# Ranks of weight splits and output sums, the first weights' engines, the attention output loads and three buffers of a hybrid decoder layer

## The chip, the cores and the metric

The kernel runs on one core of one Trainium2 chip. The metric is the device time of one execution in microseconds (us); the time before is the median of three runs. Engines are named as in the profile: PE (TensorE matmuls, PEld its weight loads), DVE (VectorE), ACT (ScalarE), POOL (GpSimd), SP (SyncE, which issues nearly all DMAs).

## What is computed

One decoder layer on 1024 tokens of width 1024, in float32:

```
h = rmsnorm(x); proj = h @ w_in
fox:  8 heads x 64, causal softmax(q k / 8 + F[t] - F[s]) v,  F = cumsum(log sigmoid(f + bias))
sb:   8 heads x 64, weights sigmoid(z) * prod over s<j<t of (1 - sigmoid(z_j)),  z = q k / 8, s < t
x = x + [rmsnorm(o_fox), rmsnorm(o_sb)] @ w_out
u = causal depthwise conv (width 3) of rmsnorm(x) @ w_up;  gate, val = split(u)
x = x + (silu(gate) * val) @ w_down;  out = rmsnorm(x)
```

## The kernel before, in words

Everything is held transposed, features on the 128 partitions and tokens along the row. A float32 operand is split into a rounded high part and the rest (`hi`, `lo`), and each product is three matmuls (`mm3`, L159 to L162): high by high, and the two mixed ones.

**Order of work.** Tile's scheduler orders the instructions of PE, DVE, ACT and POOL from their ranks (their place in the program, unless a rank is given) and its own estimate of when each can start. The order of SP is that of the program. Each engine then runs its list strictly in order; the chip's times only decide how long each entry waits.

**Start** (span 0 to 45 us). Eight 128x1024 blocks of x are loaded (`xr`), ACT makes their high part `xh` (L352) and squares them (L358, L361), DVE makes the low part `xl` (L353) and adds the squares to `sqa` (L362). PE multiplies them with the first two weight units (`w_qk[0]`, `w_qk[1]`, in four pieces each) into four PSUM banks of 12 matmuls per block; column sums of `sqa` (L180) give the norm `rst` and, spread over the rows (L185), `rbc`. `constants()` makes an identity and two masks on POOL, cast by DVE (L87, L93, L96); the second mask is written over the first one's tile.

**Weights.** Class `W` (L124 on) loads a unit into one of two `wraw` buffers and splits it piece by piece: high part on POOL (L142), low part on POOL (L144), or ACT and DVE for units with `act=True` (the last of w_out and the first of w_up). `wspl` has three pairs for the results.

**Attention** (45 to 650 us) goes head by head, in the order p, hb; `attention_stream` issues the scores, transposes and value products of a head, and between them `fill_stream` issues projection work for later heads (`v_quarter`, `qk_unit`) at a fixed rate. A head's q, k high, k low and v come back from DRAM in `load_head` (L432, L435) and `load_v` (L440) one head ahead. In a fox head DVE combines scores with a row `fbt` (L476), ACT exponentiates (L486) and POOL scales (L490). In a stick-breaking head ACT takes two sigmoids (L481 into `qt`, L482), DVE scans `qt` backwards (L494), POOL multiplies (L495). The two `qt` tiles come from the pool of the `fbt` rows (two buffers), and POOL sets their last column (L460). `finish` (L540 on) stores a pair's output to `od` and adds its squares to `oacc` on POOL (L555).

**Output projection.** After the last unit (p = 7) `open_out` (L620 on) spreads the fox norm, and loads the four fox outputs back through `load_og`: a load into a buffer `oraw` (L613; tag `hl`, two buffers, shared with the projection's `hl`), a high part on ACT (L617), a low part on DVE (L618). After a pause of 12 units of the fill's clock `fox_out` (L641 on) multiplies them with w_out while the last heads run; per row block m it loads a block of x into `xin` (L646; also tag `hl`), and DVE scales, adds (L653, L654) and stores (L655). Then come the rest of the output projection, the norm, the two large products of the feed-forward part (650 to 1400 us) and the last norm.

Of the kernel before, what the change touches and what calls it, by code (L numbers as in the profile page):

```python
# [9 lines left out]
F32 = mybir.dt.float32  # L10
# [3 lines left out]
ALU = mybir.AluOpType  # L14
# [3 lines left out]
P = 128  # L18
D = 1024
T = 1024  # L20
# [32 lines left out]
ORDER, ORDER_LAST = (0, 1, 3, 2), (0, 1, 3, 2)  # L53
LAG, LEAD, RATE, PAUSE, TRC = 3, 40.0, 1.327, 12.0, 0.67
UA = 3

PARTS = ((0, 512), (512, 256), (768, 256))
NORM_AT = ((1, 3), (2, 3), (3, 0))
# [5 lines left out]
def f32(ap):  # L64
    return ap.bitcast(F32)
# [3 lines left out]
def layer(ctx, tc, xT, wqk, wv0, wv, wout, wup, wdn, cols, fbias, yT):  # L69
# [44 lines left out]
    class W:  # L114
# [16 lines left out]
        def split(self, upto):  # L131
            if self.done == 0 and upto > 0:
                self.dma()
                self.hi = self.pool.tile([P, self.n if self.own else 1056], F32R, name=self.tag + "h")
                self.lo = self.pool.tile([P, self.n if self.own else 1056], F32R, name=self.tag + "l")
            while self.done < upto:
                q = self.n // self.pieces
                sl = slice(self.done * q, (self.done + 1) * q)
                if self.act:
                    nc.scalar.copy(self.hi[:, sl], self.raw[:, sl])  # L140
                else:
                    nc.gpsimd.tensor_scalar(self.hi[:, sl], self.raw[:, sl], 1.0, 0.0, ALU.mult, ALU.add)  # L142
                eng = nc.vector if self.act else nc.gpsimd
                eng.tensor_tensor(self.lo[:, sl], self.raw[:, sl], f32(self.hi[:, sl]), ALU.subtract)  # L144
                self.done += 1

        def get(self):
# [248 lines left out]
    ps_s = attn.enter_context(tc.tile_pool(name="ps_s", bufs=3, space=PSUM))  # L396
    ps_t = attn.enter_context(tc.tile_pool(name="ps_t", bufs=2, space=PSUM))
    ps_o = attn.enter_context(tc.tile_pool(name="ps_o", bufs=1, space=PSUM))
    NQ = 2
    oacc = bcp.tile([P, T], F32, name="oacc")  # L400
    qi = []
# [48 lines left out]
    def score(p, hb, i, ws):  # L450
        fox = p < NFOX
        q, kh, kl, vt, fbt = heads[p, hb]
        n = (i + 1) * P
        w = pp.tile([P, T], F32, name="w")
        ws[i] = w
        m = None
        if not fox:
            if len(qi) < NQ:
                qi.append(fp.tile([P, T + 1], F32, name="fbt"))
                nc.gpsimd.memset(qi[-1][:, T:T + 1], 1.0)  # L460
            qt = qi[count[0] % NQ]
            count[0] += 1
        for c0, cn in CHUNKS[i]:
            s = ps_s.tile([P, 512], F32, name="s")
            qb = q[:, i * P:(i + 1) * P]
            diag = c0 <= i * P < c0 + cn
            nc.tensor.matmul(s[:, :cn], qb, kh[:, c0:c0 + cn], start=True, stop=False)  # L467
            nc.tensor.matmul(s[:, :cn], qb, kl[:, c0:c0 + cn], start=False, stop=not diag)
            if diag:
                o = i * P - c0  # L470
                nc.tensor.matmul(s[:, o:o + P], identb, mask_f if fox else mask_s,  # L471
                                 start=False, stop=True)
            un = min(cn, n - c0)
            if fox:
                m2 = small.tile([P, 1], F32, name="m")
                nc.vector.tensor_tensor_reduce(  # L476
                    out=w[:, c0:c0 + un], in0=s[:, :un], in1=fbt[:, c0:c0 + un], scale=-1.0,
                    scalar=3.0e38 if m is None else m, op0=ALU.add, op1=ALU.min, accum_out=m2)
                m = m2
            else:  # L480
                act(qt[:, T - n + c0:T - n + c0 + un], s[:, :un], AF.Sigmoid, scale=-1.0)  # L481
                act(w[:, c0:c0 + un], s[:, :un], AF.Sigmoid)  # L482

        if fox:
            l = small.tile([P, 1], F32, name="l")
            act(w[:, :n], w[:, :n], AF.Exp, scale=-1.0, bias=m, accum_out=l)  # L486

            def rest():
                nc.vector.reciprocal(l, l)  # L489
                nc.gpsimd.tensor_scalar(w[:, :n], w[:, :n], l, 1.0, ALU.mult, ALU.mult)  # L490
        else:
            def rest():
                rev = slice(T - 1, T - n - 1 if n < T else None, -1)
                nc.vector.tensor_tensor_scan(qt[:, rev], qt[:, rev], qt[:, rev], 1.0, ALU.mult, ALU.bypass)  # L494
                nc.gpsimd.tensor_tensor(w[:, :n], w[:, :n], qt[:, T - n + 1:T + 1], ALU.mult)  # L495
        defer(0, rest)
# [42 lines left out]
    def finish(p):  # L539
        ot = heads["o", p]  # L540
        g = 0 if p < NFOX else 1

        def go():
            if p < NPAIR - 1:
                nc.sync.dma_start(od[p], ot)
            else:
                load_og(p)
            if p % NFOX == 0:
                act(oacc, ot, AF.Square)
                return  # L550
            sq = pp.tile([P, T], F32, name="osq", tag="w")
            act(sq, ot, AF.Square)
            eng = nc.vector if p == NPAIR - 1 else nc.gpsimd
            for sl in (slice(0, 512), slice(512, T)):
                eng.tensor_tensor(oacc[:, sl], oacc[:, sl], sq[:, sl], ALU.add)  # L555
            if p == NFOX - 1:
                defer(12, partial(sums, oacc, ps_p, "pj"))
            elif p == NPAIR - 1:
                fill["sums"] = partial(sums, oacc)

        def sums(sq, pool, nm):
            pss = pool.tile([P, 512], F32, name=nm)
            col_sums(pss, sq, TB)
            rsqrt_mean(rg[g], pss[:, :TB], TB, D // 2)
        defer(0, go)
# [55 lines left out]
    def open_out():  # L621
        xpool.close()
        fill["ogs"] = osx.enter_context(tc.tile_pool(name="ogs", bufs=1, side="right"))
        fill["ogp"] = ogf.enter_context(tc.tile_pool(name="ogp", bufs=1, side="right"))
        group_spread(0, rbc, ps_p, "pj")
        fill["og"] = {}
        for p in range(4):
            load_og(p)

    def out_step(part, m, c, k, ps):  # L630
        og = fill["og"]
# [8 lines left out]
    def fox_out():  # L640
        box = {}  # L641

        def step(m, c, k):
            if c == 0 and k == 0:
                box["x"] = stg.tile([P, T], F32, name="xin", tag="hl")
                nc.sync.dma_start(box["x"], xT[m * P:(m + 1) * P, :])  # L646
            if k == 0:
                box["p"] = ps_p.tile([P, 512], F32, name="pj")
            w, sl = out_step(0, m, c, k, box["p"])
            w.ahead(((m % 2) * 8 + c * 4 + k + 1) / 16)  # L650
            if k == 3:
                t = stg.tile([P, 512], F32, name="t1", tag="full")
                nc.vector.tensor_tensor(t, box["p"], rbc[:, sl], ALU.mult)  # L653
                nc.vector.tensor_tensor(t, box["x"][:, sl], t, ALU.add)  # L654
                nc.sync.dma_start(x2d[m][c], t)  # L655
# [6 lines left out]
    def fill_stream():  # L662
# [8 lines left out]
            yield from qk_unit(2 * p + 1)  # L671
            yield 0, partial(fill.__setitem__, "ready", p)
        yield 0, open_out
        yield PAUSE, lambda: None
        yield from fox_out()

    fs = fill_stream()
# [603 lines left out]
```

## Time and profile before

| | |
|---|---|
| median of 3 runs | 1425.86 us (1425.01 to 1426.44) |
| the profiled execution's own time | 1431.94 us |
| its span in the profile | 1430.2 us |
| PE, DVE, POOL, ACT busy | 92%, 78%, 54%, 43% of the span |
| mean granted TensorE clock | 0.965 |

How to read it: the span is what the profile covers of the one execution; its own time also holds 1.7 us around it. Times of rows count from the start of the span. Profiled executions and plain runs differ by more than the three plain runs do among each other, so differences are formed within the profile and then applied to the median. A busy share is an average over stages with different limits.

### The profile page before, as it was taken

How to read it: one execution, taken by the hardware profiler on the slowest of the kernel's cores; microseconds unless marked ns; L12 is line 12 of the kernel's file. 1: busy time of each engine (PE TensorE's matmuls, PEld its weight loads, DVE VectorE, ACT ScalarE, POOL GpSimd, SP SyncE). 2: the span in 40 equal slices, each digit the busy share in tenths (PEclk: the TensorE clock that was granted, in tenths of full speed). 3: DMA queues.
4: the chain of work that ended last, by engine and by line, in shares of the span. 5: the costliest groups of instructions: out<-in, count | busy, mean ns of one | idle time of the engine just before them, and what ended most of it. 6: DMA issues, size and time to landing. Idle time of an engine off the chain costs nothing.

```text
span 1430.2 us, 19128 instructions
## 1 busy us (share of the span) xinstructions
PE 1310.7 (92%) x6640; PEld 1075.8 (75%) x6640; DVE 1111.7 (78%) x1638; ACT 620.7 (43%) x1128; POOL 773.8 (54%) x680
## 2 busy tenths in 40 slices
PE   7999999999898886789989999999999989999895
PEld 5878878887687765678766788888888867878684
DVE  6246655655677677787889999988888899899987
ACT  5134434444554455354454433443433453444334
POOL 7343454445657583540004788778787774554423
PEclk9999999999999999899979999999999999999997
DMA  5555455644544455546521222333322365444303
GB/s 180 182 161 175 131 154 159 189 135 119 161 112 141 118 143 143 170 128 221 205 81 67 91 98 106 111 111 111 110 96 96 96 219 206 163 147 152 114 30 118
DMA packets 97232, 194.88 MB, mean 136 GB/s; under 512 B 8681, under 2 KB 35689, under 8 KB 97137
## 3 DMA queue, kind: packets, MB, share of 16 engines
q1 hardware_dynamic: 96272, 193.04, 42.9%
q8 instruction: 52, 0.85, 0.3%
q10 hardware_dynamic: 864, 0.64, 0.1%
q14 instruction: 44, 0.35, 0.1%
HBM read 132.79 MB, written 60.85 MB: 135 GB/s over the span
## 4 chain that ended last, share of the span: by engine, by line
PE 49%; DVE 18%; DMA 17%; POOL 6%; issue 5%; ACT 2%; SPq 2%; DVEq 0%; POOLq 0%; ACTq 0%
PE u L161 7%; PE u L162 7%; PE u L160 7%; PE pj L160 5%; PE pj L162 5%; PE pj L161 5%; DMA q<-qkd 4%; DVE fbt L494 3%; DMA vd<-vs 3%; DMA st<-td 2%; PE tp L506 2%; PE o L527 2%; DVE wl L910 2%; DMA wraw<-in_wv_dram 2%; PE o L526 1%
## 5 line engine op out<-in xcount | busy, mean ns | idle before, releaser
L881 POOL TENSOR_TENSOR s<-wraw 128x512 f32<-128x512 f32 (+1 forms) x32 | 52.7, 1647 | 213.9 <-DMA wraw<-in_wup_dram 141.3
L495 POOL TENSOR_TENSOR w<-w,fbt 128x128 f32<-128x128 f32 (+3 forms) x64 | 91.2, 1434 | 90.9 <-DVE fbt L494 59.8
L908 ACT CAST wh<-s 128x512 fp32r<-128x512 f32 (+1 forms) x136 | 79.5, 591 | 122.4 <-POOL s L882 69.8
L494 DVE TENSOR_TENSOR_SCAN fbt<-fbt 128x128 f32<-128x128 f32 (+3 forms) x64 | 102.9, 1616 | 27.9 <-ACT fbt L481 24.2
L142 POOL TENSOR_SCALAR wh<-wraw 128x256 fp32r<-128x256 f32 (+1 forms) x112 | 55.4, 511 | 111.7 <-DMA wraw<-in_wqk_dram 58.8
L506 PE MATMUL tp<-ident,w 128*128 128x128 f32 x576 | 93.2, 280 | 24.1 <-DVE pl L515 10.7
L160 PE MATMUL pj<-xh,wh 128*128 128x512 f32 x224 | 102.1, 456 | 3.7 <-DVE yf L294 3.7
L506 PEld LDWEIGHTS tp<-ident,w 128*128 128x128 f32 x576 | 70.2, 143 | 43.2 <-DVE pl L515 14.3
L910 POOL TENSOR_TENSOR wl<-wraw,wh 128x512 fp32r<-128x512 f32 x58 | 100.0, 1730 | 0.0
L515 DVE TENSOR_TENSOR pl<-tp,ph 128x512 fp32r<-128x512 f32 x96 | 64.9, 685 | 40.1 <-ACT ph L514 39.7
L162 PE MATMUL pj<-xh,wl 128*128 128x512 f32 x224 | 90.6, 404 | 0.0
L161 PE MATMUL pj<-xl,wh 128*128 128x512 f32 x224 | 90.3, 403 | 0.0
L486 ACT ACTIVATE w<-w,m 128x128 f32<-128x128 f32 (+3 forms) x64 | 49.7, 776 | 92.0 <-DVE m L476 86.9
L144 POOL TENSOR_TENSOR wl<-wraw,wh 128x256 fp32r<-128x256 f32 (+1 forms) x112 | 89.1, 814 | 0.3
L1007 DVE SCALAR_TENSOR_TENSOR tg<-ua,col,tg 128x1023 f32<-128x1023 f32 (+1 forms) x44 | 89.1, 2026 | 0.0
L908 ACT CAST wh<-wraw 128x512 fp32r<-128x512 f32 (+1 forms) x96 | 55.2, 590 | 70.0 <-DMA wraw<-in_wdn_dram 27.4
L481 ACT ACTIVATE fbt<-s 128x512 f32<-128x512 f32 (+2 forms) x96 | 47.6, 496 | 86.7 <-PE s L471 40.2
L490 POOL TENSOR_SCALAR w<-w,l 128x128 f32<-128x128 f32 (+3 forms) x64 | 48.0, 755 | 61.5 <-DVE l L489 31.0
L278 PE MATMUL pj<-wh,xh 128*128 128x256 f32 (+1 forms) x256 | 78.5, 307 | 0.8 <-DVE yf L294 0.8
L514 ACT CAST ph<-tp 128x512 fp32r<-128x512 f32 x96 | 55.6, 589 | 53.9 <-PE o L526 34.1
L910 POOL TENSOR_TENSOR wl<-s,wh 128x512 fp32r<-128x512 f32 x44 | 73.4, 1668 | 9.4 <-ACT wh L908 9.2
L467 PE MATMUL s<-kh,q 128*128 128x256 f32 (+2 forms) x192 | 69.5, 364 | 8.4 <-DMA kh<-qkd 6.4
(366 smaller groups left out, 4520.0 us busy)
## 6 DMA issues: line engine op xcount, KB each, us to landing
wraw<-in_wup_dram SPq DMA_DIRECT2D x47, 512.0 KB, 3.7
st<-td SPq DMA_DIRECT2D x74, 256.0 KB, 4.1
qkd<-hl SPq DMA_DIRECT2D x32, 512.0 KB, 3.2
td<-tg SPq DMA_DIRECT2D x44, 256.0 KB, 2.3
vd<-vs SPq DMA_DIRECT2D x32, 256.0 KB, 4.6
q<-qkd SPq DMA_DIRECT2D x16, 512.0 KB
kh<-qkd SPq DMA_DIRECT2D x32, 256.0 KB, 16.5
kl<-qkd SPq DMA_DIRECT2D x32, 256.0 KB, 17.3
```

The source lines that it names most:

```text
L144: eng.tensor_tensor(self.lo[:, sl], self.raw[:, sl], f32(self.hi[:, sl]), ALU.subtract)
L160: nc.tensor.matmul(ps, ah, bh, start=start, stop=False)
L161: nc.tensor.matmul(ps, ah, bl, start=False, stop=False)
L162: nc.tensor.matmul(ps, al, bh, start=False, stop=stop)
L278: nc.tensor.matmul(ps[:, :n], xh[k][:, sl], h, start=(k == 0), stop=False)
L467: nc.tensor.matmul(s[:, :cn], qb, kh[:, c0:c0 + cn], start=True, stop=False)
L494: nc.vector.tensor_tensor_scan(qt[:, rev], qt[:, rev], qt[:, rev], 1.0, ALU.mult, ALU.bypass)
L495: nc.gpsimd.tensor_tensor(w[:, :n], w[:, :n], qt[:, T - n + 1:T + 1], ALU.mult)
L506: nc.tensor.transpose(tp[:, a * 256 + b * P:a * 256 + (b + 1) * P], ws[2 * g + b][:, kb * P:(kb + 1) * P], ident)
L908: nc.scalar.copy(h[:, o:o + w], src)
L910: eng.tensor_tensor(l[:, o:o + w], src, f32(h[:, o:o + w]), ALU.subtract)
L1007: nc.vector.scalar_tensor_tensor(t[:, s:], us[:, :T - s], col[:, cw + tap:cw + tap + 1], t[:, s:], op0=ALU.mult, op1=ALU.add)
```

## The change

A constant `GIVE = 60` is new. (1) The splits of weights by POOL are given a rank 60 places later than their place in the program. (2) The first two units, `index < 2`, are split by ACT and DVE in place of POOL, at their own rank. (3) The two POOL additions to `oacc` get the later rank too. (4) The two `qt` tiles, and (5) `xin`, get buffers of their own in a new pool `own` (one buffer each; `xin` had two, shared). (6) The four `load_og` calls leave `open_out`; each comes after a quarter of the pause.

```diff
+GIVE = 60
...
             while self.done < upto:
...
-                if self.act:
-                    nc.scalar.copy(self.hi[:, sl], self.raw[:, sl])
-                else:
-                    nc.gpsimd.tensor_scalar(self.hi[:, sl], self.raw[:, sl], 1.0, 0.0, ALU.mult, ALU.add)
-                eng = nc.vector if self.act else nc.gpsimd
-                eng.tensor_tensor(self.lo[:, sl], self.raw[:, sl], f32(self.hi[:, sl]), ALU.subtract)
+                first = self.act or self.index < 2
+                with tc.high_priority(offset=0 if first else -GIVE):
+                    if first:
+                        nc.scalar.copy(self.hi[:, sl], self.raw[:, sl])
+                    else:
+                        nc.gpsimd.tensor_scalar(self.hi[:, sl], self.raw[:, sl], 1.0, 0.0, ALU.mult, ALU.add)
+                    eng = nc.vector if first else nc.gpsimd
+                    eng.tensor_tensor(self.lo[:, sl], self.raw[:, sl], f32(self.hi[:, sl]), ALU.subtract)
...
+    own = attn.enter_context(tc.tile_pool(name="own", bufs=1))
...
-                qi.append(fp.tile([P, T + 1], F32, name="fbt"))
+                qi.append(own.tile([P, T + 1], F32, name=f"qi{len(qi)}"))
...
-            for sl in (slice(0, 512), slice(512, T)):
-                eng.tensor_tensor(oacc[:, sl], oacc[:, sl], sq[:, sl], ALU.add)
+            with tc.high_priority(offset=0 if p == NPAIR - 1 else -GIVE):
+                for sl in (slice(0, 512), slice(512, T)):
+                    eng.tensor_tensor(oacc[:, sl], oacc[:, sl], sq[:, sl], ALU.add)
...
         fill["og"] = {}
-        for p in range(4):
-            load_og(p)
...
-                box["x"] = stg.tile([P, T], F32, name="xin", tag="hl")
+                box["x"] = own.tile([P, T], F32, name="xin")
...
         yield 0, open_out
-        yield PAUSE, lambda: None
+        for p in range(4):
+            yield PAUSE / 4, partial(load_og, p)
         yield from fox_out()
```

Lines of the changed kernel are 2 to 6 higher than those before. Three places show what it moves.

**The start, on DVE** (xl and sqa as above; `wl_` is the low part of the first weights). Before:

```order
L353 SCALAR_TENSOR_TENSOR xl_240<-xr_263,col,xh_232 128x512 x2
L353 SCALAR_TENSOR_TENSOR xl_241<-xr_270,col,xh_233 128x1024
L362 TENSOR_TENSOR sqa<-sqa,sq 128x1024
L87 CAST identb<-ident 128x128
L93 CAST mask_f<-maskw 128x128
L353 SCALAR_TENSOR_TENSOR xl_242<-xr_273,col,xh_234 128x1024
L362 TENSOR_TENSOR sqa<-sqa,sq 128x1024
L96 CAST mask_s<-maskw 128x128
L353 SCALAR_TENSOR_TENSOR xl_243<-xr_276,col,xh_235 128x1024
```

Now:

```order
L357 SCALAR_TENSOR_TENSOR xl_240<-xr_263,col,xh_232 128x512
L148 TENSOR_TENSOR wl<-wraw,wh 128x256 x2
L357 SCALAR_TENSOR_TENSOR xl_240<-xr_263,col,xh_232 128x512
L357 SCALAR_TENSOR_TENSOR xl_241<-xr_270,col,xh_233 128x1024
L366 TENSOR_TENSOR sqa<-sqa,sq 128x1024
L148 TENSOR_TENSOR wl<-wraw,wh 128x256 x2
L357 SCALAR_TENSOR_TENSOR xl_242<-xr_273,col,xh_234 128x1024
L148 TENSOR_TENSOR wl<-wraw,wh 128x256 x2
L366 TENSOR_TENSOR sqa<-sqa,sq 128x1024
L357 SCALAR_TENSOR_TENSOR xl_243<-xr_276,col,xh_235 128x1024
L148 TENSOR_TENSOR wl<-wraw,wh 128x256 x2
```

and behind the last `sqa`:

```order
L366 TENSOR_TENSOR sqa<-sqa,sq 128x1024
L89 CAST identb<-ident 128x128
L95 CAST mask_f<-maskw 128x128
L173 TENSOR_SCALAR rs_v<-p_454 128x8
L98 CAST mask_s<-maskw 128x128
L175 RECIPROCAL rs_s<-rs_s 128x8
```

Eight low parts of weights have come between the `xl` and `sqa` steps, and the three casts of constants have gone behind the last of them. On PE, before, the column sums stand ahead of the eighth block's twelve products:

```order
L162 MATMUL p_378<-xh_238,wl 128x512
L180 MATMUL p_454<-ones,sqa 128x1 x8
L160 MATMUL p_366<-xh_239,wh 128x512
L161 MATMUL p_366<-xl_247,wh 128x512
L162 MATMUL p_366<-xh_239,wl 128x512
L160 MATMUL p_370<-xh_239,wh 128x512
```

Now four of the twelve come first:

```order
L166 MATMUL p_378<-xh_238,wl 128x512
L164 MATMUL p_366<-xh_239,wh 128x512
L165 MATMUL p_366<-xl_247,wh 128x512
L166 MATMUL p_366<-xh_239,wl 128x512
L164 MATMUL p_370<-xh_239,wh 128x512
L184 MATMUL p_454<-ones,sqa 128x1 x8
L165 MATMUL p_370<-xl_247,wh 128x512
```

**The loads of fox outputs, on SP** (`od_111` to `od_114` are the outputs of fox pairs 0 to 3; 105 and 106 are q and k of pair 7). Before:

```order
L239 DMA qkd_106<-hl 128x2x512 x2
L613 DMA oraw<-od_111 128x1024
L613 DMA oraw<-od_112 128x1024
L613 DMA oraw<-od_113 128x1024
L613 DMA oraw<-od_114 128x1024
L432 DMA q<-qkd_105 128x1x1024
L435 DMA kh<-qkd_106 64x1024 x2
L435 DMA kl<-qkd_106 64x1024 x2
L440 DMA vt<-vd_110 128x8x128
L646 DMA xin<-in_xT_dram 128x1024
```

Now:

```order
L243 DMA qkd_106<-hl 128x2x512 x2
L619 DMA oraw<-od_111 128x1024
L619 DMA oraw<-od_112 128x1024
L437 DMA q<-qkd_105 128x1x1024
L440 DMA kh<-qkd_106 64x1024 x2
L440 DMA kl<-qkd_106 64x1024 x2
L445 DMA vt<-vd_110 128x8x128
L619 DMA oraw<-od_113 128x1024
L619 DMA oraw<-od_114 128x1024
L650 DMA xin<-in_xT_dram 128x1024
```

The third and fourth load have changed places with the five loads of the next head; no other row of SP has moved. On PE the third output's products (`ogh_5940` before, `ogh_6056` now) stood before the next head's scores (128x256); before:

```order
L160 MATMUL pj<-ogh_5940,wh 128x512
L467 MATMUL s<-kh,q 128x512
L468 MATMUL s<-kl,q 128x512
L161 MATMUL pj<-ogl_5941,wh 128x512
L162 MATMUL pj<-ogh_5940,wl 128x512
```

Now they stand behind those scores, and the fourth's (`ogh_6113`) behind them:

```order
L472 MATMUL s<-kh,q 128x384
L473 MATMUL s<-kl,q 128x384
L476 LDWEIGHTS identb
L476 MATMUL s<-mask_s,identb 128x128
L531 MATMUL o<-ph,vt 128x256
L511 MATMUL tp<-ident,w 128x128 x4
L532 MATMUL o<-pl,vt 128x256
L531 MATMUL o<-ph,vt 128x256
L532 MATMUL o<-pl,vt 128x256
L511 MATMUL tp<-ident,w 128x128 x3
L531 MATMUL o<-ph,vt 128x256
L532 MATMUL o<-pl,vt 128x256
```

The third output's first two products follow directly on these rows; so twelve products of the first row block have gone behind twelve rows of attention work that came after them.

**The ranked work, on POOL**, at the first score blocks of the second to last head (`w` and `fbt`, now `qi`: the attention weights and scanned row). Before:

```order
L495 TENSOR_TENSOR w<-w,fbt 128x128
L142 TENSOR_SCALAR wh<-wraw 128x256 x2
L144 TENSOR_TENSOR wl<-wraw,wh 128x256
L495 TENSOR_TENSOR w<-w,fbt 128x256
L144 TENSOR_TENSOR wl<-wraw,wh 128x256
L142 TENSOR_SCALAR wh<-wraw 128x256 x2
L144 TENSOR_TENSOR wl<-wraw,wh 128x256 x2
L555 TENSOR_TENSOR oacc<-oacc,osq 128x512 x2
L495 TENSOR_TENSOR w<-w,fbt 128x384
```

Now:

```order
L500 TENSOR_TENSOR w<-w,qi_4101 128x128
L500 TENSOR_TENSOR w<-w,qi_4112 128x256
L146 TENSOR_SCALAR wh<-wraw 128x256 x2
L148 TENSOR_TENSOR wl<-wraw,wh 128x256 x2
L146 TENSOR_SCALAR wh<-wraw 128x256 x2
L148 TENSOR_TENSOR wl<-wraw,wh 128x256 x2
L561 TENSOR_TENSOR oacc<-oacc,osq 128x512
L500 TENSOR_TENSOR w<-w,qi_4101 128x384
L561 TENSOR_TENSOR oacc<-oacc,osq 128x512
```

One `w` has passed a split and one an `oacc`. This is the only place where a `w` passes anything on POOL; elsewhere only high parts of a weight pass low parts of the same weight. What stands after 770 us in the old trace is in the same order on every engine.

## Rows read from the trace of the kernel before

**Rows 1.** Busy time by stretch: length, PE, PEld, DVE, ACT, POOL, PEclk, DMA share, GB/s

```profile
15.00:30.00 15.00, 12.38 (x52) 9.57 (x52) 15.00 (x13) 9.73 (x10) 14.83 (x11) 1.00 0.37 134
500.00:600.00 100.00, 79.70 (x434) 63.58 (x432) 75.99 (x86) 50.95 (x106) 58.66 (x52) 0.93 0.54 151
850.00:1000.00 150.00, 150.00 (x646) 121.54 (x646) 135.62 (x122) 60.92 (x85) 121.95 (x75) 1.00 0.31 106
```

**Rows 2.** Timeline of the start: start us, us, engine, line, operation [idle before <-releaser]

```profile
14.24 0.76 DVE L93 CAST mask_f<-maskw 128x128 bf16<-128x128 f32 x1 [0.57 <-POOL maskw L91]
17.36 0.42 DVE L96 CAST mask_s<-maskw 128x128 bf16<-128x128 f32 x1
...
32.99 1.95 PE L180 MATMUL p<-ones,sqa 128*128 128x1 f32 x16 [0.92 <-DVE sqa L362]
...
35.41 0.20 DVE L171 RECIPROCAL rs_s<-rs_s 128x8 f32<-128x8 f32 x1 [0.28 <-ACT rs_s L170]
...
39.22 1.03 PE L185 MATMUL p<-ident,rst 128*128 128x128 f32 x8
```

**Rows 3.** Line L353, 0 to 40 us: durations ns min/median/max, starts, forms

```profile
L353 DVE SCALAR_TENSOR_TENSOR xl<-xr,col,xh x9: 752/1426/1776, 4.7 to 29.8; 128x1024 fp32r<-128x1024 f32 x7, 128x512 fp32r<-128x512 f32 x2
```

**Rows 4.** Line L144 (split's low part on POOL), 0 to 45 us, the same columns

```profile
L144 POOL TENSOR_TENSOR wl<-wraw,wh x16: 725/757/1741, 6.9 to 40.9; 128x256 fp32r<-128x256 f32 x8, 128x264 fp32r<-128x264 f32 x8
```

**Rows 5.** Groups by shape on DVE, 600 to 700 us: busy, mean ns, idle before

```profile
L144 DVE TENSOR_TENSOR wl<-wraw,wh 128x512 fp32r<-128x512 f32 x14 | 9.4, 685 | 1.9 <-ACT wh L140 1.9
```

**Rows 6.** Timeline of SP, 533 to 560 us (issues of one line merged)

```profile
533.09 10.80 SPq L613 DMA_DIRECT2D oraw<-od  x4
543.99 0.54 SPq L432 DMA_DIRECT2D q<-qkd  x1
544.57 1.11 SPq L435 DMA_DIRECT2D kh<-qkd  x2
...
547.01 0.59 SPq L440 DMA_DIRECT2D vt<-vd  x1
549.82 9.64 SPq L646 DMA_DIRECT2D xin<-in_xT_dram  x1
```

**Rows 7.** Line L613: what SP waited (ns) at its issues, and landing time

```profile
L613 SPq EVENT_SEMAPHORE  x7: 17/17/2280, 533.0 to 646.2; - x7
...
DMA to landing us min/median/max: 3.5/3.8/4.0
```

**Rows 8.** Timeline of ACT, DVE and PE around the wait for a head's keys

```profile
538.98 1.15 ACT L617 ACTIVATE ogh<-oraw,col 128x1024 fp32r<-128x1024 f32 x1 [1.62 <-DMA oraw<-od]
...
540.16 1.28 DVE L618 SCALAR_TENSOR_TENSOR ogl<-oraw,col,ogh 128x1024 fp32r<-128x1024 f32 x1 [1.28 <-ACT ogh L617]
...
562.94 1.09 PE L467 MATMUL s<-kh,q 128*128 128x256 f32 x3 [6.40 <-DMA kh<-qkd]
...
575.40 0.28 PE L526 MATMUL o<-ph,vt 128*128 128x256 f32 x1
```

**Rows 9.** The chain that ended last, 540 to 610 us: start us, us, what

```profile
545.09 17.64 DMA kh<-qkd
...
569.89 2.00 DVE t L654 x2
...
583.84 18.14 DMA x2d<-t
```

**Rows 10.** DMA issues of the whole run: count, size of each, median us to landing

```profile
x2d<-t SPq DMA_DIRECT2D x16, 256.0 KB, 2.3
```

**Rows 11.** Timeline of ACT, 636 to 650 us: a later load of `oraw`

```profile
641.45 1.16 ACT L617 ACTIVATE ogh<-oraw,col 128x1024 fp32r<-128x1024 f32 x1 [2.48 <-DMA oraw<-od]
```

**Rows 12.** Timeline of POOL: the output sums in the last head

```profile
580.44 2.98 POOL L555 TENSOR_TENSOR oacc<-oacc,osq 128x512 f32<-128x512 f32 x2 [3.72 <-ACT osq L552]
```

**Rows 13.** Timeline of POOL: the first setting of a scan tile's last column

```profile
308.08 0.10 POOL L460 MEMSET fbt<- 128x1 f32 x1 [3.30 <-DVE m L476]
...
320.55 0.78 POOL L142 TENSOR_SCALAR wh<-wraw 128x256 fp32r<-128x256 f32 x2 [10.13 <-DMA wraw<-in_wqk_dram]
```

## The prediction

> **What bounds the kernel.** I read the busy time by stretch first. From 850 to 1000 us PE is busy for all 150.00 us [rows 1]: nothing that other engines do better there can shorten it, and the change leaves that part in its order. Time can be won in two places, where PE waits. At 15 to 30 us DVE is busy for 15.00 of 15 us and PE for 12.38; at 500 to 600 us PE works 79.70 of 100 us [rows 1]. For each I then read the timeline and the releasers of PE's waits.
>
> At the start PE waits 0.92 us at 32.99 for DVE's last `sqa`, then forms the column sums in 1.95 us, and reaches the spread of the norm at 39.22 without another wait, its list being full [rows 2]. So DVE's chain of `xl` and `sqa` steps sets the end of the start. At 562.94 PE has waited 6.40 us for the keys of the next head [rows 8]; these are on the chain that ended last, with 17.64 us of transfer from 545.09, and `x2d` with 18.14 us from 583.84 [rows 9]. SP shows why the keys are late: the four loads of fox outputs take it from 533.09 to 543.89, since two buffers serve four loads, and q, the keys and v stand behind them [rows 6].
>
> The sum is made against the profiled execution (1431.94 us, span 1430.2), which took 6.1 us more than the median; I subtract its differences from the median, 1425.86. A measurement of this kernel can tell about 0.2%, 2.85 us, from no change: faster is under 1423.0, slower above 1428.7.
>
> **The start (part 2).** *Removed from DVE ahead of the last `sqa`:* three casts. One took 0.76 us and waited 0.57 before it, one took 0.42 [rows 2]; the third (`identb`) has the shape of the first, so 0.76: 2.5 us in all. *Added:* eight low parts of 128x256. DVE's low part of 128x512 takes 0.685 us [rows 5]; half the columns are between 0.34 and 0.685, so 2.7 to 5.5 us; I take 2.7, since DVE's `xl` of 128x512 and 128x1024 also go about with the columns (752 to 1426 ns) [rows 3]. *Gained:* `xl` takes 1.43 us in the middle and up to 1.78 [rows 3], POOL's low part 0.725 to 1.741 [rows 4], long where both engines work. With the first splits off POOL, some three of the early steps should keep to the short value, 0.35 us less each: 1.1. DVE's last `sqa` ends near 31.9 instead of 32.9. *Behind it:* before, twelve products stood between sums and spread; 39.22 less 34.94 is 0.36 us each. Four now go ahead of the sums, into PE's wait: 0.36 x 4 = 1.4. Spread at 39.2 - 1.0 - 1.4 = 36.8, rounded up to 37.2, as POOL's splits of w_v now fall later, beside the last `sqa`: **-2.0 us**. From +1.5 (low parts at 0.685, no collision avoided) to -3.5 (a start two steps freer).
>
> What is late next: a mask's cast has gone between `rs_v` and the reciprocal (35.41 [rows 2]) on DVE, and waits for POOL's mask, which waits for DVE's other cast and for w_v's splits ahead of it. The two casts put the reciprocal at 34.5 to 35.5: covered by PE's products until 37. If POOL ends its splits 2 us later, the cover is gone, and this term is zero. ACT gets eight casts, some 3 us, and was busy for 9.73 of 15 [rows 1].
>
> The Trainium skill ("SBUF — State Buffer", section "Who interferes with whom") says that a VectorE instruction with two inputs in SBUF and a GpSimd instruction that reads SBUF exclude one another for the whole instruction. The trace agrees in direction (0.725 alone, up to 1.741 beside DVE); by that rule the collision only moves to w_v's splits, and the 1.1 us would be nothing: 1419.5 in place of the sum below.
>
> **The order of loads (part 6).** q goes right behind the second load. That load's issue had the 2.28 us wait [rows 7], so it ends near 535.8; q and the first keys follow at the old spacing (543.99 to 545.09) [rows 6], so the second keys start to move at 536.7 instead of 545.09. With the same 17.64 us [rows 9] they land at 554.3 instead of 562.7: PE's wait loses its 6.40 us, and what it waited for is 8.4 us earlier.
>
> What is late next is the third and fourth load. Their issue waits for the first two low parts: the first ends at 540.16 + 1.28 = 541.44 [rows 8], the second released the fourth issue near 543.6. Before, they landed in 3.5 us [rows 7]. Now they stand behind 2 MB of q, keys and v on the queue. Bounds for their landing: 3.8 us after issue at best (545.3, 547.4); at worst as `x2d`, which was issued right after v and took 18.14 us where 2.3 is its median [rows 9, 10]: 541.5 + 18.7 = 560.2 for the third. I take 558 and 560, nearer the worst end, because there too 2 MB were in front; `xin`, next behind v before, shows SP itself held for 9.64 us at its issue [rows 6]. From the fourth landing at 560: high part 1.15 on ACT, low part 1.28 on DVE [rows 8], partly queued, so 563.7; then two scalings and two `pl` at 0.685 [rows 5], two additions in 2.00 [rows 9], some 1.5 between PE and DVE: 570.0 for the value product that started at 575.40 [rows 8], that is -5.4. On PE twelve products of the first row block now follow twelve rows of attention, so attention is not held by the late loads until ACT reaches the casts ahead of its next sigmoids. **-5.0 us**, from -9 (late loads come early) to +3.6 (first rival).
>
> The same skill ("DMA: Bandwidth & Descriptors", section "Queues, rings and completion order") says that each DMA engine takes the descriptors of a queue in ring order. `x2d`'s 18.14 us [rows 9] against 2.3 [rows 10] agrees; the rule speaks against this step, since it puts the third load behind everything issued ahead of it, and by it alone the third would land with v.
>
> **Own tiles (parts 4, 5).** The one wait that I find for `xin`'s old buffer is at 641.45, 2.48 us on ACT for a load of `oraw` [rows 11]: -0.5, from 0 to -1.5. A single `xin` buffer costs nothing: the next load stands behind the store of the same block on SP in either version. POOL's settings of the last column waited 3.30 us for a `fbt` buffer, but POOL then idled 10.13 us for weights [rows 13]: 0, to -1.
>
> **Ranks (parts 1, 3).** They move one `w` past a split and one past half an `oacc`, on POOL alone. A split is worth up to 1.74 [rows 4], the half up to 2.98/2 = 1.5 [rows 12]; the `x2d` transfer from 583.84 [rows 9] ends later than either can act. 0, from -1.3 to +0.8. Nothing of the sum hangs on ranks.
>
> Sum: -2.0 - 5.0 - 0.5 = **-7.5**; profiled 1424.4, median **1418.4**.
>
> **Rivals.** *The late loads hold the middle (slower).* If the third lands at 560.2 and the fourth not with it but 9.64 us later, by another hold of SP as at `xin` [rows 6] (569.8), low part, scalings and additions as above put the value product at 579 instead of 575.4: +3.6; with -2.0 at the start +1.6, and with the next head's keys queued behind, up to +4: 1427.5 to 1430, taken as 1429. For it: two buffers and one queue. It turns the middle into a loss when the fourth lands after about 565.5, the whole after 567.5. Against: no row shows a 512 KB load 23 us behind its issue. 0.08.
>
> *The gain is given back at the next head.* `x2d` from 583.84 and the 18.14 us behind the next keys [rows 9] stay at their time, if their issue hangs on the last output store and on POOL rather than on what came earlier. Then only the start counts: -2, 1423.9, no change. For it: POOL waited 3.72 us for ACT at 580.44 [rows 12]. Against: every wait of that stretch follows from PE's list. 0.14.
>
> *The late loads are not late.* They land 3.8 us after issue, as all did [rows 7]: the middle gives the whole -8.4 or slightly more, in sum -12, 1413.5. For it: queue depth at 541 us is what four issues in sequence leave, and q may have gone by then. Against: `x2d`. 0.12.
>
> *The change does not do what it says*: of the ranks that is nearly so, priced at 0 above.
>
> **How the numbers follow.** The forecast has 0.66: 1418.4, its own bounds (-11 to -4, some ends of terms together) 1414 to 1422. The range takes in all but the outermost tenth at each side: from 1410.5 (third rival with the start's best end) to 1426 (the second rival with the start's worse end). Faster 0.66 + 0.12 = 0.78; same 0.14; slower 0.08.
>
> **What would show it.** In the changed profile: the spread at about 37 and the reciprocal before 36; PE's wait for keys near 556 under 1 us; the third `ogh` at 558 to 560, its wait put down to the load; the value product at about 570; the `x2d` transfer still about 18 us long, but some 7 us earlier; from 770 us on the same durations, shifted. I am wrong if the third load lands by 547, or the fourth after 565, or if the shift at 590 us is gone by 610.

## The result, and the profile after

The changed kernel takes 1419.32 us against 1426.15 for the kernel before it in the same runs: ratio 0.9950, 95% interval 0.9928 to 0.9973, so -7.1 us with a range of -3.9 to -10.3. Taken once more in more rounds it gave 0.9945 (0.9930 to 0.9960), -7.8 us. Forecast were 1418.4 us and -7.5, range 1410.5 to 1426. 1419.32 us is the median of six executions; one of the six took 2521.35 us, which nothing here explains, and the ratio leaves it out. The sum was right; its two large terms were not, and their errors cancelled: that is luck.

The profiled execution took 1420.63 us, span 1418.8: 11.4 us less than the span of before. The trace shows more than the runs do, because the profiled execution of before lay 6 us above its median and this one 1.3 us above its own. So I read places and mechanisms from the traces, and sizes from the ratios.

**The stretches** (as [rows 1]: length, PE, PEld, DVE, ACT, POOL, PEclk, DMA share, GB/s), of the changed kernel:

```profile
15.00:30.00 15.00, 15.00 (x70) 12.35 (x68) 15.00 (x15) 11.09 (x11) 8.56 (x6) 1.00 0.38 136
500.00:600.00 100.00, 80.44 (x422) 63.60 (x420) 77.02 (x86) 49.83 (x105) 60.59 (x52) 0.91 0.56 163
```

PE went from 12.38 to 15.00 busy us in 15 to 30, and from 79.70 to 80.44 in 500 to 600. The first place is full now; the second hardly changed, though all of it comes earlier.

**The start**, in the timeline of the changed kernel and in the groups of its two lines of steps (`xl`, now L357, and `sqa`, now L366; ns min/median/max):

```profile
L357 DVE SCALAR_TENSOR_TENSOR xl<-xr,col,xh x9: 750/1278/1428, 4.7 to 26.3; 128x1024 fp32r<-128x1024 f32 x7, 128x512 fp32r<-128x512 f32 x2
L366 DVE TENSOR_TENSOR sqa<-sqa,sq x7: 1216/1218/1420, 11.2 to 27.7; 128x1024 f32<-128x1024 f32 x7
```

```profile
12.31 0.76 DVE L148 TENSOR_TENSOR wl<-wraw,wh 128x256 fp32r<-128x256 f32 x2
...
27.68 1.42 DVE L366 TENSOR_TENSOR sqa<-sqa,sq 128x1024 f32<-128x1024 f32 x1
...
32.45 0.19 DVE L175 RECIPROCAL rs_s<-rs_s 128x8 f32<-128x8 f32 x1
...
29.47 1.84 PE L184 MATMUL p<-ones,sqa 128*128 128x1 f32 x16
...
34.45 1.06 PE L189 MATMUL p<-ident,rst 128*128 128x128 f32 x8 [1.17 <-DVE rst L180]
...
21.44 6.59 POOL L146 TENSOR_SCALAR wh<-wraw 128x264 fp32r<-128x264 f32 x4 [19.70 <-DMA wraw<-in_wv_dram]
```

`xl` has a median of 1278 ns in place of 1426 [rows 3]. The spread stands at 34.45 in place of 39.22 [rows 2], and now waits 1.17 us for DVE's `rst`. POOL idles for 19.70 us before 21.44, when w_v has landed.

**The middle.** SP, then ACT and PE in the timeline, then the chain that ended last, of the changed kernel (as [rows 6], [rows 8], [rows 9]):

```profile
527.12 3.12 SPq L619 DMA_DIRECT2D oraw<-od  x2
...
530.93 1.30 SPq L440 DMA_DIRECT2D kh<-qkd  x2
...
534.50 12.45 SPq L619 DMA_DIRECT2D oraw<-od  x2
```

```profile
553.51 1.15 ACT L623 ACTIVATE ogh<-oraw,col 128x1024 fp32r<-128x1024 f32 x1 [0.53 <-DMA oraw<-od]
...
555.70 1.17 ACT L623 ACTIVATE ogh<-oraw,col 128x1024 fp32r<-128x1024 f32 x1
...
549.41 0.35 PE L472 MATMUL s<-kh,q 128*128 128x256 f32 x1 [1.45 <-DMA kh<-qkd]
551.12 0.58 PE L473 MATMUL s<-kl,q 128*128 128x256 f32 x1 [1.36 <-DMA kl<-qkd]
561.51 0.50 PE L164 MATMUL pj<-ogh,wh 128*128 128x512 f32 x1 [1.11 <-DVE t L657]
566.36 0.28 PE L531 MATMUL o<-ph,vt 128*128 128x256 f32 x1
593.77 0.80 PE L164 MATMUL pj<-ogh,wh 128*128 128x512 f32 x1 [5.43 <-DVE t L657]
```

```profile
534.50 18.98 DMA oraw<-od
...
574.20 18.80 DMA x2d<-t
```

and the wait behind `x2d` in the trace of before:

```profile
602.74 0.80 PE L160 MATMUL pj<-ogh,wh 128*128 128x512 f32 x1 [3.28 <-DVE t L653]
```

The wait of 6.40 us for keys has become 1.45 and 1.36. In its place on the chain stands the third load, with 18.98 us. The `x2d` transfer is as long as before (18.80 for 18.14 us); behind it PE waits 5.43 us, where it was 3.28.

How the shift grows: the scans of the heads run 6.0 us earlier than before from 370 to 540 us, 10.5 us earlier at 574 (the scan of 128x896, 574.30 for 584.81), and 8.6 us at 604 (603.83 for 612.43). Of the 6.0 us, 4.8 stand at the spread of the norm. The rest is not to be put down to the start: in the trace of part 6 alone (below), whose spread is the old one (38.94), the scans from 370 to 540 us also come 2.5 to 3.7 us earlier than before. One place where these traces differ by themselves is 127.1 to 130.6 us: the granted clock is 0.50 there in the trace of before, and 1.00 in that of part 6 alone. The middle gives 4.5 at 574 us, of which 1.9 are given back by the next head.

### The profile page after: what moved, and what is told of

The parts are those of the page before. It is cut to its first block, busy times and chain, and to the rows that moved or that the text cites. A ratio compares the mean times of both kernels' runs of the same rounds, so it can differ in the third digit from the quotient of the medians.

```text
span 1418.8 us, 19128 instructions
## 1 busy us (share of the span) xinstructions
PE 1306.7 (92%) x6640; PEld 1074.8 (76%) x6640; DVE 1113.8 (79%) x1646; ACT 622.8 (44%) x1136; POOL 759.5 (54%) x664
## 4 chain that ended last, share of the span: by engine, by line
PE 53%; DMA 17%; DVE 16%; POOL 6%; issue 4%; ACT 2%; SPq 2%; DVEq 0%; POOLq 0%; ACTq 0%
PE u L165 8%; PE u L166 8%; PE u L164 8%; PE pj L164 5%; PE pj L166 5%; PE pj L165 5%; DMA q<-qkd 4%; DVE qi L499 3%; DMA vd<-vs 2%; PE tp L511 2%; PE o L532 2%; DMA oraw<-od 2%; PE pj L282 1%; PE pj L284 1%; PE pj L283 1%
## 5 line engine op out<-in xcount | busy, mean ns | idle before, releaser
L500 POOL TENSOR_TENSOR w<-w,qi 128x128 f32<-128x128 f32 (+3 forms) x64 | 94.2, 1482 | 79.9 <-DVE qi L499 41.8
L499 DVE TENSOR_TENSOR_SCAN qi<-qi 128x128 f32<-128x128 f32 (+3 forms) x64 | 104.0, 1633 | 27.7 <-ACT qi L486 24.9
L146 POOL TENSOR_SCALAR wh<-wraw 128x256 fp32r<-128x256 f32 (+1 forms) x104 | 51.3, 512 | 124.4 <-DMA wraw<-in_wv_dram 51.0
L486 ACT ACTIVATE qi<-s 128x512 f32<-128x512 f32 (+2 forms) x96 | 47.5, 494 | 86.7 <-PE s L476 41.0
L148 POOL TENSOR_TENSOR wl<-wraw,wh 128x256 fp32r<-128x256 f32 (+1 forms) x104 | 78.0, 772 | 0.2
L1012 DVE SCALAR_TENSOR_TENSOR tv<-ub,col,tv 128x1023 f32<-128x1023 f32 (+1 forms) x44 | 73.9, 1680 | 2.3 <-ACT tv L1010 2.1
```

The costliest lines, as they stand in the source:

```text
L1012: nc.vector.scalar_tensor_tensor(t[:, s:], us[:, :T - s], col[:, cw + tap:cw + tap + 1], t[:, s:], op0=ALU.mult, op1=ALU.add)
```

## The experiments

**Each part alone.** The kernel before, with nothing but part 2:

```diff
-                if self.act:
+                first = self.act or self.index < 2
+                if first:
...
-                eng = nc.vector if self.act else nc.gpsimd
+                eng = nc.vector if first else nc.gpsimd
```

> The kernel before with part 2 alone: the first two units split by ACT and DVE. Theory (DVE's steps at the start were held back by POOL's splits, and go short once these are gone): the whole of the shift at the start, spread near 34.5 instead of 39.22, DVE steps of 1.2 to 1.3 us up to 22 us, and a median of about 1421 (-5 us). Rival (the start was priced right at -2 us, and the rest of what the changed kernel shows there comes from its other parts, such as the scan tiles set ahead of the splits on POOL): spread near 37, median about 1424. The wait for keys near 557 stays at about 6 us in both.

Measured: 0.9966 (0.9951 to 0.9981), -4.9 us; 1422.9 median. PE in its timeline:

```profile
35.15 1.06 PE L186 MATMUL p<-ident,rst 128*128 128x128 f32 x8 [0.89 <-DVE rst L177]
...
555.24 1.09 PE L468 MATMUL s<-kh,q 128*128 128x256 f32 x3 [7.71 <-DMA kh<-qkd]
```

The theory holds: spread at 35.15, steps of 1.21 to 1.28 us up to 23.9, and the keys are waited for as before (7.71 us). The start's term of -2.0 was too small.

With nothing but part 6 (the four calls of `load_og` out of `open_out`, one after each quarter of the pause):

> The kernel before with part 6 alone: the four loads one at a time, the last two behind the next head's loads; xin still shares its two buffers with them. Theory (the middle gains from the keys alone): no change at the start, the wait for keys of 6.4 us falls under 2 us, the third output's high part waits for its load, and the median is about 1423 (-3 us). Rival (the middle needs xin's own tile as well, since xin, the third and the fourth load then compete for two buffers behind late loads): the first block's adds come later and the median is 1426 (no change) or more.

Measured: 0.9981 (0.9969 to 0.9993), -2.7 us; 1425.28. The timeline:

```profile
38.94 1.04 PE L185 MATMUL p<-ident,rst 128*128 128x128 f32 x8
...
551.24 0.35 PE L467 MATMUL s<-kh,q 128*128 128x256 f32 x1 [0.96 <-DMA kh<-qkd]
553.05 0.39 PE L468 MATMUL s<-kl,q 128*128 128x256 f32 x1 [1.45 <-DMA kl<-qkd]
...
558.00 0.33 SPq L644 DMA_DIRECT2D xin<-in_xT_dram  x1
```

The theory holds: the start is as before, the waits for keys are 0.96 and 1.45 us, 2.4 together, and the third `ogh` waits 0.81 us for its load. `xin` does go later (558.00, behind a low part that frees its buffer); the ratio doesn't say whether that costs anything.

With nothing but parts 4 and 5 (own tiles):

> The kernel before with parts 4 and 5 alone: own tiles for the scan rows and xin. Theory: -0.5 us, not to be told from no change, 1425.5 median; the start as before (spread 39.2) and the wait for keys as before (6.4 us). Rival (own tiles carry part of the shift at 540 us, since POOL no longer waits for a fbt buffer in the first scanned head): -1 to -2 us, to be seen as a shift of the scans from 350 us on.

Measured: 1.0004 (0.9987 to 1.0021). No change to be told from the -0.5 that was forecast; the rival's 1 to 2 us from 350 us on aren't in its trace (scans 0.1 to 0.4 us earlier from 350 to 535 us).

The changed kernel without the ranks:

```diff
-GIVE = 60
+GIVE = 0
```

> The changed kernel with GIVE = 0, so without parts 1 and 3. Theory (ranks move almost nothing): the same time as the changed kernel, 1419 within 1 us. Rival (the scans' products passing a split matter once the loads are late): slower than the changed kernel by 1 to 2 us, from 550 us on.

Measured: 0.9933 (0.9917 to 0.9948). To put the two side by side, the changed kernel in as many rounds:

> The changed kernel itself once more, in more rounds, to set it beside the same kernel without ranks (ratio 0.9933 to before). Theory (ranks are worth nothing): ratio 0.993 to 0.9945, within 1.5 us of the kernel without them. Rival (ranks cost 2 us): ratio 0.995 or more again.

Measured: 0.9945 (0.9930 to 0.9960). The intervals overlap: no gain from the ranks is seen; whether they cost a microsecond stays open. -4.9, -2.7 and nothing for the rest make -7.6, so within their intervals the parts add up to the whole.

**What the start gained from.** Twelve subtractions on a scratch tile put back a load on POOL that reads SBUF:

```diff
...
+        nc.gpsimd.memset(scr, 0.0)
+        for i in range(12):
+            nc.gpsimd.tensor_tensor(scq, scr, scr, ALU.subtract)
```

> The changed kernel, with twelve subtractions of 128x512 on POOL at the start, on a scratch tile that nobody reads: work that isn't in the reference, to put back the load on POOL that the first splits were. Theory (DVE's steps of two inputs are held back while POOL works on SBUF too): these steps go from 1.22 and 1.28 back to 1.4 to 1.8 us, the spread from 34.45 to 37 or later, the time up by 2 to 5 us, to 1421 to 1424. Rival (the gain of the start came from the casts that moved behind and from the sums' place): steps stay at 1.2 to 1.3 us while POOL works, spread at 34.5, time as the changed kernel, 1419.

and 24 fillings one that only writes:

```diff
...
+        nc.gpsimd.memset(scr, 0.0)
+        for i in range(24):
+            nc.gpsimd.memset(scq, 0.0)
```

> The changed kernel, with 24 fillings of 128x512 with zero on POOL at the start, on the same scratch tile: POOL works, but reads nothing. Theory (what collides is POOL's reading, as the Trainium skill's page SBUF State Buffer, section Who interferes with whom, has it): DVE's steps stay at 1.2 to 1.3 us, spread at 34.5, time 1419. Rival (any POOL work on SBUF holds DVE back): steps of 1.4 us and more wherever a filling runs beside them.

Measured: 0.9972 (0.9956 to 0.9988), 1424.38, with reading; 0.9956 (0.9936 to 0.9976), 1420.73, with writing. The timeline with reading (POOL's last eight subtractions run from 6.21 to 17.70):

```profile
1.45 1.04 POOL L358 TENSOR_TENSOR scq<-scr 128x512 f32<-128x512 f32 x1
...
6.21 11.49 POOL L358 TENSOR_TENSOR scq<-scr 128x512 f32<-128x512 f32 x8
...
12.38 2.06 DVE L371 TENSOR_TENSOR sqa<-sqa,sq 128x1024 f32<-128x1024 f32 x1
14.36 2.44 DVE L148 TENSOR_TENSOR wl<-wraw,wh 128x256 fp32r<-128x256 f32 x2
16.72 2.05 DVE L362 SCALAR_TENSOR_TENSOR xl<-xr,col,xh 128x1024 fp32r<-128x1024 f32 x1
...
38.97 1.06 PE L189 MATMUL p<-ident,rst 128*128 128x128 f32 x8 [1.38 <-DVE rst L180]
```

and with writing (18 fillings from 4.51 to 14.97):

```profile
4.51 10.46 POOL L358 MEMSET scq<- 128x512 f32 x18
...
9.53 1.28 DVE L362 SCALAR_TENSOR_TENSOR xl<-xr,col,xh 128x1024 fp32r<-128x1024 f32 x1 [1.23 <-ACT xh L361]
10.73 1.22 DVE L371 TENSOR_TENSOR sqa<-sqa,sq 128x1024 f32<-128x1024 f32 x1
11.87 0.76 DVE L148 TENSOR_TENSOR wl<-wraw,wh 128x256 fp32r<-128x256 f32 x2
...
33.46 1.06 PE L189 MATMUL p<-ident,rst 128*128 128x128 f32 x8 [0.23 <-DVE rst L180]
```

Beside reading, `sqa` takes 2.06 us (more than the 1.8 expected) and a pair of low parts 2.44; beside writing 1.22 and 0.76, as with an idle POOL. The spread goes back to 38.97, or stays at 33.46. So the collision is the mechanism, and it is POOL's reading. The run with reading is 4.0 us faster than the kernel before, where the changed kernel is 7 to 8: it gives up most of what the start was worth alone (4.9). The Trainium skill's page "SBUF — State Buffer" (section "Who interferes with whom") agrees with both runs.

**Why the late loads are late.** The third and fourth load issued on ACT's own queue:

```diff
-            nc.sync.dma_start(raw, od[p])
+            (nc.scalar if p in (2, 3) else nc.sync).dma_start(raw, od[p])
```

> The changed kernel, with the third and fourth load of fox outputs issued by ACT on its own queue. Theory (they are late, 19 us after issue, because they stand behind 2 MB of q, keys and v on SP's queue): now they land within 10 us of their issue, the third before 545 instead of 553.5, xin is issued earlier as well, and the time falls by 1 to 3 us against the changed kernel, to 1417. Rival (the 16 engines are full from 531 to 553 whichever queue is used): landing stays near 550, the keys come later by as much, and the time is 1419 to 1421.

Measured: 1.0012 (0.9998 to 1.0025), 1428.76, all of the gain lost. ACT and PE in the timeline:

```profile
533.48 0.39 ACTq L619 DMA_DIRECT2D oraw<-od  x1
...
543.18 1.15 ACT L623 ACTIVATE ogh<-oraw,col 128x1024 fp32r<-128x1024 f32 x1 [6.52 <-DMA oraw<-od]
544.24 0.58 ACT L486 ACTIVATE qi<-s 128x512 f32<-128x512 f32 x1
...
548.46 0.33 ACTq L619 DMA_DIRECT2D oraw<-od  x1
...
556.22 1.15 ACT L623 ACTIVATE ogh<-oraw,col 128x1024 fp32r<-128x1024 f32 x1 [5.37 <-DMA oraw<-od]
...
544.38 1.22 PE L164 MATMUL pj<-ogh,wh 128*128 128x512 f32 x2 [4.43 <-ACT ogh L623]
```

Half of the theory holds: on a queue of its own the third load lands 9.7 us after its issue instead of 19. The time went the other way, and both expectations missed why. The edit also changed the order that the scheduler made. ACT now has each high part ahead of sigmoids that stood before it in the changed kernel, so it stands 6.52 and 5.37 us in front of loads that take 8 to 10 us, with sigmoids (544.24) queued behind; and the fourth load is issued from ACT's own list, 15 us after the third (548.46). In this run a load that landed sooner, but was needed sooner still, was worse than a late one behind work. The queue by itself, with the old order, was not tried.

**The two later waits.** `t` in four tiles of its own (scan rows back in the pool of `fbt`, to make room):

```diff
...
-                t = stg.tile([P, 512], F32, name="t1", tag="full")
+                t = own.tile([P, 512], F32, name=f"t1{(2 * m + c) % 4}")
```

> The changed kernel, with the sums of a row block (t, which goes to x2d) in four tiles of their own in place of two shared ones, and the scan rows back in the pool of fbt. Theory (the wait of 18.8 us for x2d behind the next head's loads, at 574 to 593, is a wait for a free t): PE's wait of 5.4 us at 593.77 goes, and the time falls by 3 to 5 us, to 1414 to 1416. Rival (the next block's xin, issued by SP behind that store at 586, ends the wait in its place): PE or DVE waits there for xin, time 1418 to 1419.

Measured: 0.9926 (0.9906 to 0.9946), 1417.42, between the two and not to be told from the changed kernel. By the trace the rival holds: PE no longer waits at 593, but DVE waits for the next transfer in line, as timeline and chain show:

```profile
594.32 1.29 DVE L658 TENSOR_TENSOR t<-xin,t 128x512 f32<-128x512 f32 x2 [3.90 <-DMA xin<-in_xT_dram]
```

```profile
579.33 14.96 DMA xin<-in_xT_dram
```

So `xin` too, in two tiles and one block ahead:

```diff
...
-                box["x"] = own.tile([P, T], F32, name="xin")
-                nc.sync.dma_start(box["x"], xT[m * P:(m + 1) * P, :])
+                for i in ((0, 1) if m == 0 else (m + 1,) if m + 1 < KT else ()):
+                    box["x", i] = own.tile([P, T], F32, name=f"xin{i % 2}")
+                    nc.sync.dma_start(box["x", i], xT[i * P:(i + 1) * P, :])
+                box["x"] = box["x", m]
```

> As the kernel with four tiles for t (scan rows in the pool of fbt), and xin in two tiles of its own, the next block loaded while this one is worked on, so that it stands ahead of the next head's loads on SP. Theory (after the x2d store, xin behind the head's loads was the second transfer that ends the wait at 594): neither is waited for, DVE's wait of 3.9 us for xin goes, and the time falls by 2 to 4 us against the kernel with four tiles, to 1413 to 1415. Rival (the attention of that head paces the stretch from 575 to 605 by its scans on DVE, and the projection only fills gaps): under 1 us, 1416.5 to 1417.5.

Measured: 0.9909 (0.9888 to 0.9930), 1415.56: the fastest of all, -13.0 us against the kernel before, though its interval overlaps that of four tiles alone. `xin` now stands ahead of the next head's loads on SP, and DVE's wait is 1.21:

```profile
563.17 0.38 SPq L651 DMA_DIRECT2D xin<-in_xT_dram  x1
...
568.41 0.54 SPq L437 DMA_DIRECT2D q<-qkd  x1
...
591.91 0.69 DVE L660 TENSOR_TENSOR t<-xin,t 128x512 f32<-128x512 f32 x1 [1.21 <-DMA xin<-in_xT_dram]
```

In its trace the first scan of the last head comes at 596.66, where the changed kernel has 603.83; the output projection's next part starts at 652.84 in place of 655.76, so more than half of that was given back on the way.

The first two fox outputs early, in tiles of their own, and all four ahead of the next head's loads:

```diff
...
+            if p == NPAIR - 1:
+                for i in (0, 1):
+                    heads["raw", i] = own.tile([P, T], F32, name=f"oraw{i}")
+                    nc.sync.dma_start(heads["raw", i], od[i])
             yield from qk_unit(2 * p)
...
```

> The changed kernel (scan rows in the pool of fbt) with the first two fox outputs loaded into tiles of their own before the last projection of q and k, and the third and fourth through the two shared buffers in open_out, all ahead of the next head's loads. Theory (the third and fourth load are late only by their place behind 2 MB, and the keys were late only by SP's wait for buffers): all four outputs are there by 540, the keys wait less than 3 us, the value product of that head comes 2 to 4 us earlier than in the changed kernel, time 1416 to 1417. Rival (1 MB more ahead of the keys delays them by as much as the late loads cost): PE waits 5 us for keys, time 1419 to 1421.

Measured: 0.9929 (0.9909 to 0.9949), 1417.3. PE waits 0.72 us for keys in all:

```profile
551.67 0.36 PE L473 MATMUL s<-kl,q 128*128 128x256 f32 x1 [0.72 <-DMA kl<-qkd]
```

The value product comes at 563.86 (566.36 in the changed kernel). That doesn't settle the 2 to 4 us: the scans of this trace run 2.1 us ahead of the changed kernel's already from 427 to 462 us, before the early loads are issued (473.01), and 2.3 behind them at 533. The intervals overlap, so no gain over the changed kernel is shown.

Both together, with two tiles for `t` and one early output:

> As the kernel with two xin tiles and own tiles for t, but with two tiles for t in place of four, and one fox output loaded before the last projection; all four outputs ahead of the next head's loads. Theory: with two tiles t waits for its x2d store again behind the next head's loads, as in the changed kernel, so most of what four tiles gave is lost, 1416 to 1418. Rival (the early outputs make the first blocks end before the next head's loads): 1411 to 1413, the best of all.

Measured: 0.9960 (0.9942 to 0.9978), 1422.4, worse than either theory. PE waits 4.79 us for keys again, since three loads through two buffers keep SP from 526.27 to 534.67, and with two tiles `t` waits for its store again:

```profile
526.27 8.40 SPq L621 DMA_DIRECT2D oraw<-od  x3
```

```profile
553.43 0.55 PE L472 MATMUL s<-kh,q 128*128 128x256 f32 x1 [4.79 <-DMA kh<-qkd]
...
590.94 0.69 DVE L663 TENSOR_TENSOR t<-pj,rbc 128x512 f32<-128x512 f32 x1 [3.68 <-DMA x2d<-t]
```

## Why the prediction was right, and where not

**The start: right in kind, too small** (forecast -2.0, alone -4.9). The term that was mis-sized is "Gained: ... some three of the early steps ... 0.35 us less each: 1.1". In the traces the seven `xl` and seven `sqa` of 128x1024 add up to 21.7 us before and 18.2 after: 3.5 us. I expected w_v's splits to take the place of the first splits on POOL; but their weights land at 21.44, so four of the seven pairs of steps run beside an idle POOL, and the fifth (from 21.31) keeps 1.28 and 1.22 us as well. The other terms held: the casts were 2.5 us as stated; of eight added low parts six stood in the chain, 0.76 a pair, 2.3 us for the 2.7 taken. Together 3.7, and the last `sqa` ends near 29.1 for 32.9.

A price was misread beside it: 0.36 us for each of the twelve products between sums and spread is a mean over two clocks. Before, the granted clock was 0.50, the lower of its two levels, from 35.0 to 38.4, where nine products take 3.38 us; in the changed kernel it stays at 1.00, and the eight that are left stand 0.23 us apart (columns as [rows 1], before and now):

```profile
35.02:38.40 3.38, 3.38 (x9) 2.61 (x9) 1.00 (x6) 0.21 (x1) 1.19 (x3) 0.50 0.00 0
```

```profile
31.31:33.28 1.97, 1.97 (x8) 1.26 (x8) 1.24 (x6) 0.21 (x1) 1.97 (x6) 1.00 0.00 0
```

All three traces with the old start show this fall of the clock, behind PE's wait for `sqa` and in or after the column sums. Of the eleven with the new start one does, that with ACT's queue, and its spread still comes at 34.28. Why the clock falls was not tried. The term "0.36 x 4 = 1.4" came out near its size all the same, for another reason: from the sums' start to the spread it is now 4.98 us for 6.23, 1.25 less, and what ends it is DVE's `rst` and no longer PE's list.

The Trainium skill's rule made of this term nothing ("the collision only moves"). The rule is borne out by the two runs on POOL; the collision didn't move, because POOL was waiting for a load. Rule and row were both right, and the question that I didn't ask was when POOL would have work again.

The cover named for the reciprocal is gone, as feared: PE waits 1.17 us for `rst`. That costs little, as the reciprocal comes at 32.45, not at 34.5.

**The loads: right in kind, too large** (forecast -5.0, alone -2.7). What was forecast of the transfers came true: taken back by 6 us to the start of the trace before, keys at 555.4 (forecast 554.3), third load 559.5 (558), fourth by 561.7 (560), last low part 564.2 (563.7). The sign given for the keys, a wait under 1 us, was missed: 1.45 and 1.36. What failed is the last step, "some 1.5 between PE and DVE: 570.0". The value product came at 566.36, that is 572.4 in the old frame, -3.0 for -5.4: 8.1 us behind the end of the last low part (556.96 + 1.28), where the sum had 6.3. In the changed trace DVE, and in that of before PE:

```profile
556.96 1.28 DVE L624 SCALAR_TENSOR_TENSOR ogl<-oraw,col,ogh 128x1024 fp32r<-128x1024 f32 x1
...
560.77 1.29 DVE L657 TENSOR_TENSOR t<-pj,rbc 128x512 f32<-128x512 f32 x2
```

```profile
566.05 0.78 PE L160 MATMUL pj<-ogh,wh 128*128 128x512 f32 x1
```

The first scaling, at 560.77, lets PE begin the second row block, and from 561.51 on PE works off 18 products of it, 0.23 us each, 4.2 us, ahead of the value product. The same 18 stand ahead of it in PE's order of before; there 13 of them had run among attention rows, from 566.05 on, before PE last waited. The change had moved the twelve of the first block from PE's time before the wait for keys to behind the attention rows, and so the second block fell due later, in one piece. The scans say the same: the first three of that head come 16 to 19 us earlier than before, the fourth, behind these products, 9.4 (569.91 for 579.30). I had counted the moved rows as no cost because they leave attention free, and not where they fall due. This is read from the traces; no run puts the twelve back.

Two small slips change nothing: the bound of 560.2 adds 18.7 us where its row has 18.14, and the first rival's 579 is 579.8 by its own terms.

**What was given back**: the rival on the `x2d` transfer was true in part. The transfer is not at its old time, but 18.80 us long where it was 18.14, and PE waits longer behind it (5.43 for 3.28). The shift shrank from 10.5 to 8.6 us there. The experiments with `t` and `xin` show two transfers, one after the other, behind the next head's loads.

**Tiles and ranks**: nothing that can be told from the forecast of -0.5 and 0. The rival in which the late loads hold the middle didn't come: the fourth had landed by 561.7 in the old frame, before the 565.5 at which it decides.

So -7.5 was met although the start brought 2.9 us more than its term and the loads 2.3 less; by the middle values the prediction named the wrong part as the larger one. The intervals of the two parts (-7.0 to -2.7 and -4.4 to -1.0) overlap, so which is larger is likely and not certain; but each forecast lies outside the interval of its own part.

## What to carry to other kernels

When work is taken off one engine to free another, ask not only what collides now but when the freed engine gets its next work: a load that lands late can leave a whole stretch free. When instructions move behind a wait, add them up where they fall due; PE work that filled a wait doesn't vanish with it. And a store or load behind a 2 MB burst on the same queue took 15 to 19 us in these traces, a wait wherever its result or its buffer is needed; so order small transfers ahead of the burst, or give them buffers enough to be late.

## What was not expected of the hardware

DVE's delay beside POOL's reading doesn't grow with DVE's own size: +0.84 us on a step of 1.22, +0.77 on one of 1.28, and 1.22 instead of 0.38 for a low part of 128x256, while POOL's instruction, 1.04 alone, takes 1.44 on average. What it follows is the size of POOL's instruction: beside high parts of 128x264 (0.39 us alone) the steps take 1.42, +0.14 and +0.20; beside low parts of 128x264 (0.74 alone) 1.77 in the run with part 2 alone, +0.49 and +0.55; beside the subtractions (1.04 alone) some +0.8. That fits a DVE step that waits for one POOL instruction each time. The other way it is dearer: of the four high parts from 21.44 to 28.03 the first takes 2.57 us, while DVE makes two steps at their short values, and each of the others 1.38.
